# Segment mean of ten million sorted rows on one core: two junk tiles in turn for VectorE's products and for ScalarE's id sums

## The chip, the cores and the metric

One core of a Trainium2 chip runs the whole kernel. The metric is the device time of one execution in microseconds (us), the median of several runs. Of the engines, VectorE (DVE), ScalarE (ACT) and GpSimd (POOL) do the work; TensorE (PE) has six small matmuls; SyncE (SP) only issues transfers.

## The reference, cut to what matters

```python
data: 10,000,000 float32;  segment_ids: 10,000,000 int64, sorted, in 0..9999
sums[s]   = sum of data where segment_ids == s
counts[s] = number of rows where segment_ids == s
return sums / max(counts, 1)          # 10,000 float32
```

## The kernel before, in words

The data are laid out as 128 partitions of 78,125 rows. Each partition's stretch is cut into 90 rows of L = 875 elements, and since the ids are sorted and a segment holds some 1,000 elements, the kernel takes it that each such row holds at most one change of segment (a check at the end leads to a general path otherwise). So it need not read all ids. It needs, for each row, the place KK where the segment changes; of the first row of a pair the sum ahead of that place (A), of the second row the sum behind it (B), and the total of the pair (T). What lies between the two places is T - A - B.

The stages, which all run beside each other:

- **Loads.** SyncE's queue issues 45 data tiles `data_t` of two rows each (L225; 875 KB, 16 buffers) and, among them, probes: single ids at every 175th place (L213, L218).
- **First look** (`first_look`, L361 to L421, and for the odd pairs `bridge`, L483 to L526), on VectorE. From the probes it works out a window of ids that must hold the change, and writes its offset into IDX (L405, L521). Rows come in groups; PLAN holds for each group the step after which each of its parts runs, by hand.
- **Gathers** (`gather`, L345), on GpSimd's queue. 90 indirect transfers bring 175 or 232 ids per partition into one of 18 slots of the tile GT. Six gathers of a group go out one after the other.
- **Id sums** (`add_ids`, L431), on ScalarE. One activation over the gathered ids with an accumulator: its sum goes to GS, and the products themselves, which nobody reads, go to a junk tile. On the chip it is two instructions: ACTIVATE and ACTIVATION_READ_ACCUMULATOR.
- **Second look** (`second_look` L441, `bridged` L534), on VectorE. KK from GS.
- **Row totals** (`total`, L559), on ScalarE, the same form over both rows of a data tile: 45 of them, the accumulator to T, the unused products to `junk_a`.
- **Row splits** (`split`, L568), on VectorE. One scalar_tensor_tensor per row compares a ramp with KK, multiplies by the data and accumulates: the sum goes to A or B, and the unused products to `junk_v`. There are 90 of them, again two instructions each: SCALAR_TENSOR_TENSOR and DVE_READ_ACCUMULATOR.
- **The rest**: some 300 small VectorE operations (counts, scans, tables of the outputs, checks), some large ones on GpSimd, and a last part for the late rows (L1093 to L1159), which ends with the output's transfers (L1173).

The order on each engine is written out by hand: the main loop (L1280 to L1308) goes through the 90 splits, and behind each split it issues the small operations that PLAN and POS put there. So splits stand directly behind each other in some places and have one to thirteen small operations between them in others. Id sums and totals are laid among each other on ScalarE in the same loop. `need` and `mark` only check that order when the program is built.

The waits come from the framework: it notes what each instruction reads and writes, and lets an instruction wait on a semaphore for the earlier ones it must follow, also for those of its own engine. In the kernel before, every split writes `junk_v` from column 0 on, so each one follows the split before it; every id sum and every total (and the verdict's sum at L833) writes `junk_a` from column 0 on, so each one follows the one before it, of whichever kind.

Of the kernel before, what the change touches and what calls it, by code (L numbers as in the profile page):

```python
# [10 lines left out]
BF16 = mybir.dt.bfloat16  # L11
# [3 lines left out]
ACT = mybir.ActivationFunctionType  # L15
AX = mybir.AxisListType

P = 128
D = 78125
L = 875  # L20
# [6 lines left out]
WO = 232  # L27
# [149 lines left out]
def kernel(  # L177
# [16 lines left out]
    cpool = ctx.enter_context(tc.tile_pool(name="cpool", bufs=1))  # L194
# [37 lines left out]
    V, BT, KK, A, B = (q5[:, i, PAD:] for i in range(5))  # L232
    GT = gpool.tile([P, RING, WO], I64, name="GT")
    gt32 = GT.bitcast(I32)

    def view(ap, dims):
        return bass.AP(ap.tensor, ap.offset, [list(ap.ap[0])] + dims)

    nc.scalar.activation(  # L239
        out=gt32[:, :, 0 : 2 * WO : 2], in_=view(q5[:, 0, 0:1], [[0, RING], [0, WO]]), func=ACT.Copy  # L240
    )

# [6 lines left out]
    iota = ppool.tile([P, 1024], FP32, name="iota")  # L249
# [21 lines left out]
        out=plast, in0=pc, scalar1=float(P - 1), scalar2=1.0e6, op0=ALU.is_equal, op1=ALU.mult  # L271
# [5 lines left out]
        out=sp_i, in0=sp_i, scalar1=3, scalar2=None, op0=ALU.arith_shift_right  # L277
# [36 lines left out]
    RR = cpool.tile([P, NOD], FP32, name="RR")  # L314
    DD = cpool.tile([P, NOD], FP32, name="DD")
    uu = cpool.tile([P, 2 * NOD], FP32, name="uu")
    junk_v = cpool.tile([P, L], BF16, name="junk_v")
    junk_a = cpool.tile([P, 2 * L], BF16, name="junk_a")

    def own(t, i, j):  # L320
        return view(t[:, 4 * i : 4 * i + 1], [[4, j - i], [1, 2]])

    def odd(t, i, j):
        return view(t[:, 4 * i + 2 : 4 * i + 3], [[4, j - i], [1, 2]])
# [7 lines left out]
    slots, queue, made = {}, [], set()  # L332

    def mark(what, rows):
        made.update((what, r) for r in rows)

    def need(what, rows):
        assert all((what, r) in made for r in rows), (what, [r for r in rows if (what, r) not in made])
# [89 lines left out]
    def add_ids(r):  # L428
        mark('GS', [r])
        w = W if r % 4 < 2 else WO  # L430
        nc.scalar.activation(  # L431
            out=junk_a[:, 0:w], in_=gt32[:, slots[r], 0 : 2 * w : 2], func=ACT.Copy,
            accum_out=GS[:, r : r + 1],
        )

# [127 lines left out]
    def split(r):  # L563
        need('KK', [r])
        mark('A', [r])
        n = min(L, D - r * L)
        d = tiles[r // 2][:, (r % 2) * L : (r % 2) * L + n]
        nc.vector.scalar_tensor_tensor(  # L568
            out=junk_v[:, 0:n], in0=iota[:, 0:n], scalar=KK[:, r : r + 1], in1=d,
            op0=ALU.is_ge if r % 2 else ALU.is_lt, op1=ALU.mult,  # L570
            accum_out=(B if r % 2 else A)[:, r : r + 1],
        )
# [707 lines left out]
    for s in range(-60, NR):  # L1280
        while pnext < len(pieces) and pieces[pnext][2] <= s + X_DATA:
            f, a, _ = pieces[pnext]
            f(*a)
            pnext += 1
        while nt < NT and 2 * nt <= s + X_DATA:
            load_data(ORDER[nt])
            nt += 1
        if s == -X_DATA:
            nc.scalar.dma_start(
                out=snt[0 : P - 1, :],  # L1290
                in_=segment_ids[D : N].rearrange("(p d) -> p d", d=D)[:, 0:1],
            )
        if s == -1:
            for f in after[s][:head]:
                f()
        if s >= -1:
            for r in sums_at[s]:
                add_ids(r)
        if s == -1:
            for f in after[s][head:]:  # L1300
                f()
        if s >= 0:
            r = SEQ[s]
            for t in totals_at[s]:
                total(t)
            split(r)
            for f in after[s]:
                f()  # L1308
# [31 lines left out]
```

## Time and profile before

| | |
|---|---|
| median of 3 runs | 185.46 us (185.43, 185.46, 188.05) |
| the profiled execution | 185.97 us, of which its span is 184.2 us |
| VectorE busy | 141.4 us (77%), 479 instructions |
| ScalarE busy | 132.8 us (72%), 291 instructions |
| GpSimd busy | 115.8 us (63%), 176 instructions |
| row splits L568 | 90 x 1117 ns, and 90 reads of the accumulator x 82 ns |
| id sums L431 | 90 x 384 ns, and 90 reads x 187 ns |
| row totals L559 | 45 x 1650 ns, and 45 reads x 186 ns |
| moved by DMA | 56.69 MB, mean 308 GB/s |

Times in the rows are counted from the start of the span. A line such as L568 is the line of the kernel that issued the instruction. In a timeline, the first number is the start, the second the duration in us, and a bracket at the end is the idle time of the engine just before and what ended it. [...] A wait that ends while an earlier record of the same engine runs on doesn't show as idle.

### The profile page before, as it was taken

Reading aid. Unit: us, or ns where it says so; the run is one execution under the profiler, and the core shown is the slowest. Engines: PE = TensorE matmul, PEld = TensorE weight load, DVE = VectorE, ACT = ScalarE, POOL = GpSimd, SP = SyncE. Lnnn points to the kernel's source line nnn. Section 1 sums busy time; section 2 is a strip of 40 time slices with the busy share of each in tenths; the row PEclk is TensorE's granted clock in tenths of the full one; section 3 lists DMA queues with packets and bytes.
Section 4 is the critical chain, followed back from the end, with each engine's and each line's share of the span. In section 5 each row is a group of like instructions: output and inputs, shape, how many; then the busy total and the mean of one; then the engine's idle time right before and its main releaser. Section 6 shows DMA issues by size and latency. Waiting matters only on the chain.

```text
span 184.2 us, 1506 instructions
## 1 busy us (share of the span) xinstructions
PE 1.6 (1%) x6; PEld 1.4 (1%) x6; DVE 141.4 (77%) x479; ACT 132.8 (72%) x291; POOL 115.8 (63%) x176
## 2 busy tenths in 40 slices
PE   0000000000000000020000000000000000000100
PEld 0000000000000000020000000000000000000100
DVE  6404385820899995769967999979999999999990
ACT  8903566654899996959957949679988687996410
POOL 5476777778585776876773857468628579245700
DMA  5899999999999999999999999999999999950000
GB/s 120 118 289 263 165 251 370 299 405 338 391 351 331 372 373 342 403 254 398 347 350 395 344 350 384 364 410 412 410 405 415 414 403 412 409 240 0 0 0 12
DMA packets 47684, 56.69 MB, mean 308 GB/s; under 512 B 37664, under 2 KB 38104, under 8 KB 47671
## 3 DMA queue, kind: packets, MB, share of 16 engines
q1 hardware_dynamic: 41739, 40.32, 66.3%
q0 software_dynamic: 5760, 16.26, 25.2%
q14 instruction: 13, 0.11, 0.2%
q10 hardware_dynamic: 172, 0.00, 0.1%
HBM read 58.97 MB, written 0.04 MB: 320 GB/s over the span
## 4 chain that ended last, share of the span: by engine, by line
DMA 33%; DVE 27%; issue 25%; POOL 7%; ACT 5%; POOLq 0%; DVEq 0%; ACTq 0%
DMA GT<-in_segment_ids_dram,IDX 18%; DVE junk_v L568 15%; DMA data_t<-in_data_dram 15%; POOL GT L345 5%; ACT junk_a L431 3%; ACT junk_a L559 2%; DVE q L587 1%; DVE most L1135 1%; DVE pa L1022 0%; POOL i_i L250 0%; DVE shf L988 0%; DVE xa L998 0%; DVE FFP L887 0%; DVE bad L725 0%; DVE q L590 0%
## 5 line engine op out<-in xcount | busy, mean ns | idle before, releaser
L345 POOL DMA_INDIRECT GT<-in_segment_ids_dram,IDX x90 | 91.0, 1011 | 44.1 <-issue 26.0
L568 DVE SCALAR_TENSOR_TENSOR junk_v<-iota,q,data_t 128x875 bf16<-128x875 f32 x90 | 100.6, 1117 | 3.4 <-DMA data_t<-in_data_dram 2.7
L559 ACT ACTIVATE junk_a<-data_t 128x1750 bf16<-128x1750 f32 (+1 forms) x45 | 74.3, 1650 | 7.2 <-DMA data_t<-in_data_dram 5.1
L431 ACT ACTIVATE junk_a<-GT 128x175 bf16<-128x175 int32 (+1 forms) x90 | 34.6, 384 | 30.6 <-DMA GT<-in_segment_ids_dram,IDX 26.3
L431 ACT ACTIVATION_READ_ACCUMULATOR junk_a<-GT 128x1 f32 x90 | 16.8, 187 | 0.0
L441 DVE SCALAR_TENSOR_TENSOR q<-YY,GS 128x6 f32<-128x6 f32 (+2 forms) x9 | 1.5, 170 | 13.8 <-ACT junk_a L431 13.0
L534 DVE TENSOR_TENSOR q<-ZV,GS 128x6 f32<-128x6 f32 (+1 forms) x8 | 1.3, 160 | 10.7 <-ACT junk_a L431 10.7
L559 ACT ACTIVATION_READ_ACCUMULATOR junk_a<-data_t 128x1 f32 x45 | 8.4, 186 | 0.0
L568 DVE DVE_READ_ACCUMULATOR junk_v<-iota,q,data_t 128x1 f32 x90 | 7.4, 82 | 0.0
L361 DVE TENSOR_TENSOR q<-pr 128x12 f32<-128x12 int32 (+3 forms) x9 | 1.6, 176 | 4.8 <-DMA pr<-in_segment_ids_dram 4.8
L239 ACT ACTIVATE GT<-q 128x4176 int32<-128x4176 f32 x1 | 3.9, 3899 | 0.0
L833 ACT ACTIVATE junk_a<-bad 128x272 bf16<-128x272 f32 x1 | 0.4, 429 | 4.3 <-DVE bad L814 4.3
L1038 POOL TENSOR_TENSOR xa<-pa,RG 128x720 f32<-128x720 f32 x1 | 1.6, 1630 | 1.9 <-DVE RG L1034 1.9
L1090 POOL TENSOR_TENSOR pb<-pb,RB 128x620 f32<-128x620 f32 x1 | 1.3, 1302 | 2.4 <-DVE RB L875 2.4
L1058 POOL TENSOR_TENSOR xa<-xa 128x36 f32<-128x36 f32 (+3 forms) x5 | 2.3, 469 | 0.3
L548 POOL TENSOR_TENSOR uu<-uu,GS 128x44 f32<-128x44 f32 x1 | 0.3, 278 | 3.5 <-ACT junk_a L431 3.5
L457 POOL TENSOR_SCALAR LN<-NBP 128x6 f32<-128x6 f32 (+1 forms) x8 | 1.6, 199 | 1.2 <-issue 0.7
L464 POOL TENSOR_TENSOR FB<-FB,wb 128x6 f32<-128x6 f32 (+1 forms) x8 | 1.8, 228 | 0.7
L470 POOL TENSOR_TENSOR WV<-wb,WV 128x6 f32<-128x6 f32 (+1 forms) x8 | 1.6, 205 | 0.7
L461 POOL TENSOR_SCALAR FB<-NBP 128x6 f32<-128x6 f32 (+1 forms) x8 | 1.6, 198 | 0.6
L1025 POOL TENSOR_SCALAR pb<-pb 128x620 f32<-128x620 f32 x1 | 1.8, 1771 | 0.1
L526 DVE TENSOR_TENSOR ZV<-IDX,WV 128x6 f32<-128x6 int32 (+1 forms) x8 | 1.3, 165 | 0.7
(162 smaller groups left out, 81.3 us busy)
## 6 DMA issues: line engine op xcount, KB each, us to landing
data_t<-in_data_dram SPq DMA_DIRECT2D x44, 875.0 KB
GT<-in_segment_ids_dram,IDX POOLq DMA_INDIRECT x90
data_t<-in_data_dram SPq DMA_DIRECT2D x1, 562.5 KB
pr<-in_segment_ids_dram SPq DMA_DIRECT2D x22, 11.0 KB
pr<-in_segment_ids_dram SPq DMA_DIRECT2D x3, 6.0 KB
out_dram<-OUT SPq DMA_DIRECT2D x1, 36.6 KB
pr<-in_segment_ids_dram SPq DMA_DIRECT2D x1, 4.0 KB
snt<-in_segment_ids_dram ACTq DMA_DIRECT2D x1, 1.0 KB
```

The lines of the kernel that those rows point to most:

```text
L239: nc.scalar.activation(out=gt32[:, :, 0 : 2 * WO : 2], in_=view(q5[:, 0, 0:1], [[0, RING], [0, WO]]), func=ACT.Copy)
L345: nc.gpsimd.indirect_dma_start(out=GT[:, slots[r], 0:w], out_offset=None, in_=ids2d[:], in_offset=bass.IndirectOffsetOnAxis(ap=IDX[:, r : ...
L361: nc.vector.tensor_sub(out=BT[:, a:b], in0=VI[:, a + 1 : b + 1], in1=VI[:, a:b])
L431: nc.scalar.activation(out=junk_a[:, 0:w], in_=gt32[:, slots[r], 0 : 2 * w : 2], func=ACT.Copy, accum_out=GS[:, r : r + 1],)
L457: e.tensor_scalar(out=own(LN, i, j), in0=own(NB, i, j), scalar1=-1024.0 * FAR, scalar2=-3.0 * L, op0=ALU.mult, op1=ALU.add,)
L464: e.tensor_tensor(out=o(FB), in0=o(FB), in1=o(wb), op=ALU.add)
L559: nc.scalar.activation(out=junk_a[:, 0:n], in_=tiles[t][:, 0:n], func=ACT.Copy, accum_out=T[:, 2 * t : 2 * t + 1])
L568: nc.vector.scalar_tensor_tensor(out=junk_v[:, 0:n], in0=iota[:, 0:n], scalar=KK[:, r : r + 1], in1=d, op0=ALU.is_ge if r % 2 else ALU.is_ ...
L587: nc.vector.tensor_sub(out=odd(A), in0=even(T), in1=even(A))
L1025: e.tensor_scalar(out=o, in0=o, scalar1=0.0, scalar2=None, op0=ALU.is_equal)
L1058: nc.gpsimd.tensor_tensor(out=m[:, :, 0 : w - h], in0=m[:, :, 0 : w - h], in1=m[:, :, h:w], op=ALU.add)
L1135: nc.vector.tensor_reduce(out=most, in_=add, axis=AX.X, op=ALU.add)
```

## The change

Three things change. `junk_v` becomes two tiles of the same size, and each split takes the other one than the split before it. The id sums get two tiles of their own, `junk_i`, 232 wide, and take them in turn in the same way. The row totals (and the verdict's sum) keep `junk_a`. `turned` turns the list of two round while the program is being built and gives the first; it leaves no instruction.

```diff
+    def turned(two):
+        two.reverse()
+        return two[0]
+
...
-    junk_v = cpool.tile([P, L], BF16, name="junk_v")
+    junk_v = [cpool.tile([P, L], BF16, name=f"junk_v{k}") for k in (0, 1)]
+    junk_i = [cpool.tile([P, WO], BF16, name=f"junk_i{k}") for k in (0, 1)]
     junk_a = cpool.tile([P, 2 * L], BF16, name="junk_a")
...
         nc.scalar.activation(
-            out=junk_a[:, 0:w], in_=gt32[:, slots[r], 0 : 2 * w : 2], func=ACT.Copy,
+            out=turned(junk_i)[:, 0:w], in_=gt32[:, slots[r], 0 : 2 * w : 2], func=ACT.Copy,
             accum_out=GS[:, r : r + 1],
         )
...
         nc.vector.scalar_tensor_tensor(
-            out=junk_v[:, 0:n], in0=iota[:, 0:n], scalar=KK[:, r : r + 1], in1=d,
+            out=turned(junk_v)[:, 0:n], in0=iota[:, 0:n], scalar=KK[:, r : r + 1], in1=d,
             op0=ALU.is_ge if r % 2 else ALU.is_lt, op1=ALU.mult,
             accum_out=(B if r % 2 else A)[:, r : r + 1],
         )
```

## Rows read from the trace of the kernel before

**Rows 1.** Stretches: busy us of each engine, TensorE clock, DMA share, GB/s.

```profile
48.00:93.80 45.80, 0.99 (x4) 0.93 (x4) 38.34 (x113) 39.83 (x88) 32.60 (x47) 1.00 1.05 356
...
124.30:164.00 39.70, 0.00 (x0) 0.00 (x0) 39.00 (x141) 35.22 (x71) 23.70 (x33) 1.00 1.01 406
164.00:179.30 15.30, 0.59 (x2) 0.50 (x2) 14.97 (x34) 7.21 (x17) 7.28 (x12) 1.00 0.02 7
```

**Rows 2.** Whom VectorE waits for from 114.6 us on: total us, times, longest.

```profile
DVE q L441 <- ACT junk_a L431: 1.2, 1, 1.2
DVE junk_v L568 <- DMA data_t<-in_data_dram: 0.3, 1, 0.3
```

**Rows 3.** Timeline of VectorE: splits that wait for data.

```profile
93.77 1.13 DVE L568 SCALAR_TENSOR_TENSOR junk_v<-iota,q,data_t 128x875 bf16<-128x875 f32 x1 [1.56 <-DMA data_t<-in_data_dram]
...
101.09 1.13 DVE L568 SCALAR_TENSOR_TENSOR junk_v<-iota,q,data_t 128x875 bf16<-128x875 f32 x1 [0.92 <-DMA data_t<-in_data_dram]
...
114.51 1.13 DVE L568 SCALAR_TENSOR_TENSOR junk_v<-iota,q,data_t 128x875 bf16<-128x875 f32 x1 [0.26 <-DMA data_t<-in_data_dram]
```

**Rows 4.** Timelines of VectorE, GpSimd, ScalarE, VectorE: the chain to the last group.

```profile
109.11 0.17 DVE L405 SCALAR_TENSOR_TENSOR IDX<-ST,wb 128x6 int32<-128x6 f32 x1
...
110.04 1.08 POOL L345 DMA_INDIRECT GT<-in_segment_ids_dram,IDX  x1 [0.70 <-issue]
...
123.85 0.36 ACT L431 ACTIVATE junk_a<-GT 128x175 bf16<-128x175 int32 x1 [0.70 <-DMA GT<-in_segment_ids_dram,IDX]
...
124.34 0.17 DVE L441 SCALAR_TENSOR_TENSOR q<-YY,GS 128x6 f32<-128x6 f32 x1 [1.20 <-ACT junk_a L431]
```

**Rows 5.** Timeline of VectorE: a split behind a split, then L910.

```profile
102.15 0.08 DVE L568 DVE_READ_ACCUMULATOR junk_v<-iota,q,data_t 128x1 f32 x1
102.27 1.13 DVE L568 SCALAR_TENSOR_TENSOR junk_v<-iota,q,data_t 128x875 bf16<-128x875 f32 x1
103.32 0.08 DVE L568 DVE_READ_ACCUMULATOR junk_v<-iota,q,data_t 128x1 f32 x1
103.32 0.17 DVE L910 TENSOR_TENSOR psx<-rp,q 128x20 f32<-128x20 f32 x1
```

**Rows 6.** Timeline of VectorE: small operations, one and two between splits.

```profile
128.36 0.16 DVE L490 SCALAR_TENSOR_TENSOR LL<-LK 128x3 f32<-128x3 f32 x1
128.43 0.16 DVE L873 TENSOR_TENSOR RB<-q,ct 128x10 f32<-128x10 f32 x1
...
175.00 0.08 DVE L568 DVE_READ_ACCUMULATOR junk_v<-iota,q,data_t 128x1 f32 x1
175.00 0.15 DVE L840 TENSOR_SCALAR badi<-small 128x1 int32<-128x1 f32 x1
175.12 1.13 DVE L568 SCALAR_TENSOR_TENSOR junk_v<-iota,q,data_t 128x875 bf16<-128x875 f32 x1
```

**Rows 7.** Timeline of VectorE: the splits that are counted, first and last ones.

```profile
50.79 1.13 DVE L568 SCALAR_TENSOR_TENSOR junk_v<-iota,q,data_t 128x875 bf16<-128x875 f32 x1
...
129.68 1.13 DVE L568 SCALAR_TENSOR_TENSOR junk_v<-iota,q,data_t 128x875 bf16<-128x875 f32 x1
...
156.03 1.13 DVE L568 SCALAR_TENSOR_TENSOR junk_v<-iota,q,data_t 128x875 bf16<-128x875 f32 x1
...
173.95 1.13 DVE L568 SCALAR_TENSOR_TENSOR junk_v<-iota,q,data_t 128x875 bf16<-128x875 f32 x1
```

**Rows 8.** Timeline of ScalarE: a sum behind a sum, and a product behind a sum.

```profile
99.80 0.19 ACT L431 ACTIVATION_READ_ACCUMULATOR junk_a<-GT 128x1 f32 x1
100.02 0.36 ACT L431 ACTIVATE junk_a<-GT 128x175 bf16<-128x175 int32 x1
...
173.18 0.18 ACT L833 ACTIVATION_READ_ACCUMULATOR junk_a<-bad 128x1 f32 x1
173.28 0.34 ACT L1146 ACTIVATE add<-ga,q 128x31 f32<-128x31 f32 x1
```

**Rows 9.** DMA queue of the 90 gathers: packets, MB, share of 16 engines.

```profile
q0 software_dynamic: 5760, 16.26, 25.2%
```

## The prediction

> **What bounds the kernel now.** I read the stretches first. From 48 us to 164 us the DMA engines never rest: their share is 1.05 at 356 GB/s up to 93.8 us and 1.01 at 406 GB/s from 124.3 us on [rows 1]. The reader is to see what changes between the two: in the second stretch VectorE is busy 39.00 of 39.70 us, and from 164 us, with the DMA share down to 0.02, still 14.97 of 15.30 us. So the last 55 us, 124.3 to 179.3, are VectorE's, and the transfers end some 15 us ahead of it.
>
> Next I read whom VectorE waits for. From 114.6 us on there are two entries in all, 1.2 us for ScalarE's id sums and 0.3 us for a data tile [rows 2], whose wait began before the window. Before that it is different: at 93.77 us a split starts after 1.56 us of waiting for its data tile, at 101.09 after 0.92, and at 114.51 after 0.26 us [rows 3]. Whatever VectorE gains ahead of such a wait only makes the wait longer, as long as the data comes when it did.
>
> The 1.2 us wait ends at 124.34 us in the second look of the last group. Behind it stands a chain [rows 4]: VectorE writes the offsets IDX at 109.11 + 0.17 = 109.28 us, the first of six gathers of the group starts on GpSimd 0.76 us later, at 110.04, the others follow one by one, and the last id sum starts at 123.85 us after ScalarE had idled 0.70 us for its gather. ScalarE's own speed isn't in this wait: it was idle before the sum.
>
> **The change part by part.** No instruction is added or dropped, no step is moved and no byte is transferred more. Two junk tiles taken in turn only move the wait for a product to be overwritten: from the instruction just before to the one two before, or off the row total for ScalarE's sums.
>
> *A split right behind a split.* The read of the accumulator starts at 102.15 us, and the next split at 102.27, 0.12 us later and 0.04 us behind that read's end [rows 5]. Behind the next split the read starts at 103.32 and an instruction that needs nothing of the split, L910, at 103.32 as well. So the wait costs up to 0.12 us, nearly all of it hidden from the idle column, since the 0.08 us read counts as busy. The trace has no accumulating instruction that follows a split without such a wait, so the bounds are nothing and 0.12 us. A loss is excluded for this edit by itself: what the split waits for after the change was done before what it waits for now. I take 0.12, from L910, the only row of an instruction that follows a split unheld.
>
> [...]
>
> *A split one small operation behind a split.* At 175.00 us the read and L840 start together, the split at 175.12 [rows 6]: the wait for the read still binds. Small operations that don't wait follow at 0.07 us (128.36 to 128.43 in the same rows), so the split could start at 175.07 or 175.08; bounds nothing and 0.05 us, I take 0.04. With two or more operations between, the read is long done and nothing is gained.
>
> *How many are on the path.* In the whole trace 16 splits start 0.12 us behind the read of the split directly before them, the first at 50.79 and the last at 173.95 us; but only two of the 16, at 156.03 and 173.95, come after 124.34 us [rows 7]. There the other checks and sums fill the places between splits. Six more have one small operation between, from 129.68 us [rows 7] to 175.12 us [rows 6]. The gain on the path behind 124.34 us is 2 x 0.12 + 6 x 0.04 = 0.48 us; bounds 0 and 2 x 0.12 + 6 x 0.05 = 0.54 us.
>
> *The 14 earlier ones.* All but one lie ahead of the split that waits for data at 101.09 us or of the one at 93.77 us [rows 3], and what they give goes into those waits. The split at 102.27 us [rows 5] lies behind the last of them that matters to the chain of rows 4: IDX at 109.11 comes up to 0.12 us earlier, and so do the gathers and the wait's end at 124.34. Bounds nothing and 0.12, I take 0.10, since VectorE works without a long wait from 102.27 to 109.11 us.
>
> *ScalarE.* Today a sum starts 0.22 us behind the start of the read before it (99.80 to 100.02), while the first product of the late rows, which has no such wait, starts 0.10 us behind it (173.18 to 173.28) [rows 8]. That is 0.12 us for each sum, and for each row total behind a sum; for 90 sums and at most 44 totals up to 134 x 0.12 = 16 us of ScalarE's time, bounds nothing and that. Two totals in a row keep their wait. On the path I count it as nothing: the only wait of VectorE for ScalarE in the last 70 us ends with a sum before which ScalarE was idle [rows 2, 4]. Its cover is the gathers' landing; if that cover were gone the 1.2 us of rows 2 would be the most it could bring. Earlier, sums that end sooner let VectorE write IDX sooner and gathers start sooner; the data wait at 93.77 us takes that back.
>
> *The sum.* 0.48 + 0.10 = 0.58 us, say 0.6. The profiled execution took 185.97 us, with a span of 184.2 and 1.8 us around it, so it would take 185.4. It stands 0.5 us above the median of the runs, 185.46; on that scale the time is 185.46 - 0.6 = 184.9 us. What is late next is VectorE still: the last data is there when VectorE still has 15 us to do [rows 1], and no other engine is waited for.
>
> **The rivals.**
>
> *The hold isn't the wait (no gain).* Two accumulating instructions might not overlap with the read between them, whatever the semaphores. Then splits start 0.12 us behind the read after the change too, and only what ScalarE's 0.12 us bring is left: 185.3 to 185.5 us. For it: no row shows an unheld accumulating follower. Against it: L910 [rows 5], and that L840's follower waits as long for a read that is one operation back [rows 6]. [...]
>
> *The earlier splits count in full.* If the head weren't set by the data's coming but by VectorE's own pace, all 16 splits would count, and the two with one operation between in the head: 16 x 0.12 + 8 x 0.04 = 2.2 us, so 183.2 us. For it: VectorE also waits for id sums in the head, behind gathers that its own IDX starts, as in rows 4. Against it: 1.56 us of waiting for data at 93.77 us [rows 3], and a DMA share of 1.05 before it [rows 1], so the data can't come sooner.
>
> *Gathers go ahead of the data (slower).* With VectorE and ScalarE ahead in the head, gathers start earlier and take DMA time from the data tiles for which the splits wait at 93.77, 101.09 and 114.51 us. One gather is 16.26 MB / 90 = 0.18 MB [rows 9], which takes 0.51 us at 356 GB/s [rows 1]. Each one that comes to stand ahead of the tile of 114.51 us moves the whole VectorE stretch by 0.51 us. One such gather costs 0.1 us less than the 0.6 gained; from two on the kernel is slower, by 2 x 0.51 - 0.6 = 0.4 us: 185.9 us. For it: the DMA engines are full, so an earlier gather must displace something. Against it: VectorE's whole gain in the head is 14 x 0.12 us, under 2 us, so hardly more than one gather can come earlier, and by 114.5 us the same gathers are due in both versions.
>
> **How the numbers follow.** The forecast, 184.9 us with its own range from 184.6 to 185.3, has 0.55; no gain on VectorE, 185.4, has 0.22; the full head, 183.2, has 0.08; gathers ahead, 185.9, has 0.12; 0.03 is left for what I don't see. The range that reaches into the full head on one side and past two gathers and the scatter between the runs on the other is 183.7 to 186.2 us. A measurement of this kernel tells about 2%, 3.7 us, from no change; none of the cases reaches 181.8 or 189.2 us. So faster has 0.03, same 0.94 and slower 0.03.
>
> **What would show it.** Right: in the timeline of VectorE a split behind a split starts with the read of the accumulator or within 0.03 us of it, on ScalarE the step from a read to the next sum goes from 0.22 to about 0.10 us, and the busy time of both hardly moves while ScalarE idles more for gathers and data. The wait for data at 93.77 us grows, the second look at 124.34 us starts at about 124.2, and the last split starts 0.6 us earlier than 177.82 us. Wrong on the price: the 0.12 us stay between splits. Wrong on the place: VectorE's data waits between 93 and 115 us end earlier or later by more than 0.5 us; then the order of gathers and data set the time, and the difference between the two versions there is carried to the end.

## The result and the profile after

The changed kernel took 186.76 us, the median of 20 runs (185.61 to 188.94); the kernel before, 20 runs beside it, 185.35 us. The ratio is 1.0073 with a 95% interval from 1.0044 to 1.0101. So the change is a loss of 0.7%, some 1.4 us, inside the 2% that one would call "same", but outside the forecast's range (183.7 to 186.2 us) and with the wrong sign. A second set of runs of the changed kernel gave 1.0069. Comparisons leave disturbed (slower) runs out, and of the two experiments whose profile was disturbed, e1 and h4, no packet time is used.

The profiled execution of the changed kernel took 187.62 us, its span 185.8. The page's busy times and its DMA queues:

```profile
PE 1.6 (1%) x6; PEld 1.4 (1%) x6; DVE 140.1 (75%) x479; ACT 124.1 (67%) x291; POOL 115.9 (62%) x176
...
q1 hardware_dynamic: 41739, 40.32, 66.2%
q0 software_dynamic: 5760, 16.26, 25.8%
```

ScalarE is busy 8.7 us less than before and VectorE 1.3 us less, with the same instructions: busy time counts overlapping records once (of records that sum to 147 us before and 146 us after on ScalarE, 132.8 and 124.1 us are busy; on VectorE, of 171 and 170 us, 141.4 and 140.1), and a read of the accumulator now runs beside the instruction behind it (16 reads of 0.08 us are VectorE's 1.3 us). The prediction had said that both hardly move. The bytes and packets are the same too; but the gathers' packets (q0) took 25.8% of a longer span, 47.9 us, where [rows 9] had 25.2% of 184.2, 46.4 us.

What was forecast for the instructions is there. Timeline of VectorE, changed kernel:

```profile
95.94 1.13 DVE L573 SCALAR_TENSOR_TENSOR junk_v<-iota,q,data_t 128x875 bf16<-128x875 f32 x1 [1.41 <-DMA data_t<-in_data_dram]
...
103.19 1.13 DVE L573 SCALAR_TENSOR_TENSOR junk_v<-iota,q,data_t 128x875 bf16<-128x875 f32 x1 [0.80 <-DMA data_t<-in_data_dram]
104.25 0.08 DVE L573 DVE_READ_ACCUMULATOR junk_v<-iota,q,data_t 128x1 f32 x1
104.25 1.13 DVE L573 SCALAR_TENSOR_TENSOR junk_v<-iota,q,data_t 128x875 bf16<-128x875 f32 x1
105.30 0.08 DVE L573 DVE_READ_ACCUMULATOR junk_v<-iota,q,data_t 128x1 f32 x1
...
126.38 0.17 DVE L446 SCALAR_TENSOR_TENSOR q<-YY,GS 128x6 f32<-128x6 f32 x1 [0.87 <-ACT junk_i L436]
...
176.66 0.08 DVE L573 DVE_READ_ACCUMULATOR junk_v<-iota,q,data_t 128x1 f32 x1
176.66 0.15 DVE L845 TENSOR_SCALAR badi<-small 128x1 int32<-128x1 f32 x1
176.73 1.12 DVE L573 SCALAR_TENSOR_TENSOR junk_v<-iota,q,data_t 128x875 bf16<-128x875 f32 x1
...
180.58 0.27 DVE L1164 SCALAR_TENSOR_TENSOR OUT<-gb,q,most 128x31 f32<-128x31 f32 x1
```

The pair of [rows 5] is at 104.25 us now: the second split starts with the read of the first, where it came 0.12 us behind it. The pair with one small operation between ([rows 6], 175.00 to 175.12 us) went from 0.12 to 0.07 us (176.66 to 176.73). Timeline of ScalarE, changed kernel, the place of [rows 8]:

```profile
101.33 0.35 ACT L436 ACTIVATE junk_i<-GT 128x175 bf16<-128x175 int32 x1
101.58 0.18 ACT L436 ACTIVATION_READ_ACCUMULATOR junk_i<-GT 128x1 f32 x1
101.67 0.34 ACT L436 ACTIVATE junk_i<-GT 128x175 bf16<-128x175 int32 x1
```

A sum starts 0.09 us behind the read before it, not 0.22. And the last stretch is shorter as forecast. It begins with the second look that ended the wait of [rows 4], at 126.38 us now, and runs to the start of the last operation on the output (180.58 us): 54.20 us; before, from 124.34 us [rows 4] to 178.99 us, it took 54.65 us. (Rows 4 and the prediction call this look the last group's. It is the last but one's, of six rows; the last group's, of four rows, comes at 143.66 us in the kernel before, without a wait. The sums don't hang on the name.)

But that stretch begins 2.04 us later. The stretches that answer to [rows 1], and whom VectorE waits for, in the changed kernel:

```profile
48.00:95.97 47.97, 0.98 (x4) 0.93 (x4) 37.55 (x115) 37.02 (x89) 32.56 (x47) 1.00 1.06 358
126.38:166.00 39.62, 0.00 (x0) 0.00 (x0) 39.00 (x142) 33.13 (x70) 24.13 (x33) 1.00 1.01 404
166.00:181.00 15.00, 0.59 (x2) 0.50 (x2) 14.60 (x33) 6.82 (x17) 7.05 (x12) 1.00 0.03 14
```

```profile
DVE junk_v L573 <- DMA data_t<-in_data_dram: 5.9, 4, 3.0
```

The end is VectorE's, as before. By "the head" is meant all that lies ahead of the last stretch. There VectorE waits 5.9 us for data tiles in four waits (2.7 us in three before), but the longest of the four replaces another wait and costs nothing. Before:

```profile
74.30 0.17 DVE L534 TENSOR_TENSOR q<-ZV,GS 128x6 f32<-128x6 f32 x1 [2.77 <-ACT junk_a L431]
```

The changed kernel at the same place:

```profile
73.29 1.13 DVE L573 SCALAR_TENSOR_TENSOR junk_v<-iota,q,data_t 128x875 bf16<-128x875 f32 x1 [3.02 <-DMA data_t<-in_data_dram]
...
74.35 0.16 DVE L539 TENSOR_TENSOR q<-ZV,GS 128x6 f32<-128x6 f32 x1
```

So at 74.35 us VectorE is level with before, and the delay arises behind that: the split that waited until 93.77 us [rows 3] waits until 95.94 us. This one profile lies 0.9 us above the kernel's median, so it can't say by how much the data came late. A second profile of the same kernel (the run f4 below) took 185.31 us, 1.1 us under the median of its runs, and has the look at

```profile
124.27 0.17 DVE L446 SCALAR_TENSOR_TENSOR q<-YY,GS 128x6 f32<-128x6 f32 x1 [1.11 <-ACT junk_i L436]
```

Each profile set on its own kernel's median, an estimate, the look comes at 123.7 us before and at 125.5 and 125.4 us in the two profiles of the changed kernel, 1.7 to 1.8 us later. What can be compared from one profile to the next is the packet time: the durations of all packets in the trace, summed, over 16 engines. It was 169.2 us before, 171.7 us in this profile of the changed kernel and 170.6 us in the second one, for the same packets.

### The profile page after: what moved, and what is told of

Same layout as the page of the kernel before. It is cut to its first block, busy times and chain, and to the rows that moved or that the text cites. A ratio compares the mean times of both kernels' runs of the same rounds, so it can differ in the third digit from the quotient of the medians.

```text
span 185.8 us, 1458 instructions
## 1 busy us (share of the span) xinstructions
PE 1.6 (1%) x6; PEld 1.4 (1%) x6; DVE 140.1 (75%) x479; ACT 124.1 (67%) x291; POOL 115.9 (62%) x176
## 3 DMA queue, kind: packets, MB, share of 16 engines
q1 hardware_dynamic: 41739, 40.32, 66.2%
q0 software_dynamic: 5760, 16.26, 25.8%
## 4 chain that ended last, share of the span: by engine, by line
DMA 34%; DVE 26%; issue 19%; POOL 12%; ACT 5%; POOLq 0%; DVEq 0%; ACTq 0%
DMA GT<-in_segment_ids_dram,IDX 21%; DVE junk_v L573 17%; DMA data_t<-in_data_dram 14%; POOL GT L350 9%; ACT junk_a L564 4%; ACT junk_i L436 2%; DVE q L592 1%; DVE most L1140 1%; POOL i_i L254 0%; DVE shf L993 0%; POOLq L350 0%; POOL WV L475 0%; POOL FB L469 0%; POOL LN L462 0%; POOL FB L466 0%
## 5 line engine op out<-in xcount | busy, mean ns | idle before, releaser
L573 DVE SCALAR_TENSOR_TENSOR junk_v<-iota,q,data_t 128x875 bf16<-128x875 f32 x90 | 99.5, 1116 | 7.2 <-DMA data_t<-in_data_dram 5.9
L436 ACT ACTIVATE junk_i<-GT 128x175 bf16<-128x175 int32 (+1 forms) x90 | 33.6, 374 | 36.8 <-DMA GT<-in_segment_ids_dram,IDX 35.2
L436 ACT ACTIVATION_READ_ACCUMULATOR junk_i<-GT 128x1 f32 x90 | 16.8, 187 | 0.0
```

The lines of the kernel that those rows point to most:

```text
L436: nc.scalar.activation(out=turned(junk_i)[:, 0:w], in_=gt32[:, slots[r], 0 : 2 * w : 2], func=ACT.Copy, accum_out=GS[:, r : r + 1],)
L573: nc.vector.scalar_tensor_tensor(out=turned(junk_v)[:, 0:n], in0=iota[:, 0:n], scalar=KK[:, r : r + 1], in1=d, op0=ALU.is_ge if r % 2 else ...
```

## The experiments

Two theories. *Order*: VectorE and ScalarE are earlier in the head, so gathers and loads are issued in another order or rhythm and spoil each other (the rival of the prediction, in a larger form). *Place*: the three added tiles lie ahead of most other tiles in SBUF and move all of them by 2720 bytes. In the program as built, GT, where the gathers land, goes from byte 184576 of each partition, a multiple of 64, to 187296, 32 bytes past one; its slots are 1856 = 29 x 64 bytes apart, so all 18 are off. The 16 data buffers, 7008 bytes apart, are in turn on and 32 past a multiple of 64, and those two halves change roles.

All runs, in one table; the sections below give edits and expectations. Every kernel computes the whole of the reference. "Turned" says what takes two tiles in turn; "GT" is its start past a multiple of 64; the ratio is to the kernel before, run beside it on the same chip; the last stretch is measured as above.

| run | turned | GT | ratio [95% interval] | packet time, us | last stretch, us |
|---|---|---|---|---|---|
| before | none | 0 | 1 | 169.2 | 54.65 |
| the change | both | 32 | 1.0073 [1.0044, 1.0101] | 171.7 | 54.20 |
| e1 | none | 32 | 1.0034 [0.9997, 1.0070] | | 54.59 |
| e2 | both | 0 | 0.9988 [0.9949, 1.0028] | 169.6 | 54.09 |
| e3 | none | 32 | 1.0033 [0.9996, 1.0071] | 170.9 | 54.57 |
| e4 | both | 0 | 1.0003 [0.9963, 1.0042] | 169.6 | 54.00 |
| f1 | splits | 0 | 0.9983 [0.9951, 1.0014] | 169.0 | 54.11 |
| f2 | sums | 0 | 1.0010 [0.9973, 1.0048] | 169.3 | 54.60 |
| f3 | both, pitch 7040 | 0 | 1.0044 [1.0011, 1.0078] | 170.4 | 54.02 |
| f4 (the change again) | both | 32 | 1.0069 [1.0031, 1.0107] | 170.6 | 53.99 |
| g1 | none, pitch 7040 | 0 | 0.9954 [0.9919, 0.9989] | 168.4 | 54.59 |
| g2 | none | 0 | 1.0024 [0.9990, 1.0057] | 169.1 | 54.60 |
| g3 | none | 8 | 1.0023 [0.9994, 1.0051] | 170.0 | 54.69 |
| g4 | both, pitch 7072 | 0 | 1.0026 [0.9991, 1.0060] | 169.4 | 54.13 |
| h1 | none | 32 | 1.0073 [1.0045, 1.0101] | 171.1 | 54.65 |
| h2 | both | 0 | 1.0004 [0.9977, 1.0032] | 169.2 | 53.99 |
| h3 | splits, pitch 7040 | 0 | **0.9935 [0.9908, 0.9963]** | 168.4 | 54.07 |
| h4 | both, pitch 7040 | 0 | 0.9963 [0.9932, 0.9994] | | 54.03 |
| i1 | none | 0 | 1.0001 [0.9978, 1.0024] | 169.1 | 54.61 |
| i2 | splits, pitch 7040 | 32 | 1.0011 [0.9984, 1.0037] | 169.9 | 54.15 |

**Moving all tiles, or GT alone, by 32 bytes.** e1 (before) and e2 (the change) make `junk_a` 32 bytes wider, which moves everything behind it:

```diff
-    junk_a = cpool.tile([P, 2 * L], BF16, name="junk_a")
+    junk_a = cpool.tile([P, 2 * L + 16], BF16, name="junk_a")
```

> The kernel before with junk_a 32 bytes wider and nothing else, so that every tile allocated behind it (the data tiles, GT) lies 32 bytes further, as it does to a multiple of 64 bytes in the changed kernel; every instruction and wait as before. Address theory (the new tiles push GT from a multiple of 64 bytes to 32 bytes past one, and the gathers then take longer: 25.8% of 185.8 us against 25.2% of 184.2 in the two profiles): slower than before by about 2.0 us, the 1.4 measured and the 0.6 forecast as a gain, ratio near 1.010. Order theory (the earlier id sums and splits change the order of gathers and data, and the data of the head comes 2 us later): as before, ratio 1.000 within 0.002.

> The changed kernel with junk_a 32 bytes wider and nothing else, so that the data tiles and GT lie as in the kernel before to a multiple of 64 bytes; every instruction and wait as in the changed kernel. Address theory: the loss goes and the forecast gain is left, 0.4 to 0.6 us faster than before, ratio near 0.997. Order theory: as the changed kernel, ratio near 1.007.

e3 (before) and e4 (the change) leave 32 bytes free ahead of GT, so that GT alone moves (and the few tiles behind it):

```diff
-    GT = gpool.tile([P, RING, WO], I64, name="GT")
-    gt32 = GT.bitcast(I32)
+    GTW = gpool.tile([P, RING * WO + 4], I64, name="GT"); GT = GTW[:, 4:].rearrange("p (r w) -> p r w", w=WO)
+    gt32 = GTW.bitcast(I32)[:, 8:].rearrange("p (r w) -> p r w", w=2 * WO)
```

> The kernel before with GT alone 32 bytes further (a wider tile of which the first four ids are left unused); the data tiles and all else where they were. If GT's place is what counts: as the first of these runs, about 2 us slower, ratio near 1.010. If the data tiles' place counts, or the order: ratio 1.000 within 0.002.

> The changed kernel with GT alone 32 bytes further, which brings it back to a multiple of 64 bytes; the data tiles stay where the change put them. If GT's place is what counts: ratio near 0.997, as the second of these runs. If the data tiles' place counts, or the order: as the changed kernel, ratio near 1.007.

With GT off a multiple of 64 the kernel before got to 1.0034 and 1.0033, with intervals that just touch 1; with GT back on one the changed kernel got to 0.9988 and 1.0003. All four lean to place, and e3 and e4, where the data buffers didn't move, to GT. The size was missed: of e1 and e3 place had expected about 1.010, and a third of that came.

**One part of the change alone, GT on a multiple of 64.** f1 turns the splits alone (and widens `junk_a` by 32 bytes for GT's sake), f2 the sums alone:

```diff
 f1, against the change:
-    junk_i = [cpool.tile([P, WO], BF16, name=f"junk_i{k}") for k in (0, 1)]
-    junk_a = cpool.tile([P, 2 * L], BF16, name="junk_a")
+    junk_a = cpool.tile([P, 2 * L + 16], BF16, name="junk_a")
...
-            out=turned(junk_i)[:, 0:w], in_=gt32[:, slots[r], 0 : 2 * w : 2], func=ACT.Copy,
+            out=junk_a[:, 0:w], in_=gt32[:, slots[r], 0 : 2 * w : 2], func=ACT.Copy,
 f2, against the change:
-    junk_v = [cpool.tile([P, L], BF16, name=f"junk_v{k}") for k in (0, 1)]
+    junk_v = cpool.tile([P, L], BF16, name="junk_v")
...
-            out=turned(junk_v)[:, 0:n], in0=iota[:, 0:n], scalar=KK[:, r : r + 1], in1=d,
+            out=junk_v[:, 0:n], in0=iota[:, 0:n], scalar=KK[:, r : r + 1], in1=d,
```

> Only the splits take two junk tiles in turn; the id sums stay with junk_a, and junk_a is 32 bytes wider, so that the data tiles and GT lie as before to a multiple of 64 bytes. Address theory (the loss of the change came from GT's place alone, the waits act as forecast): the VectorE stretch from the last second look to the end is 0.5 us shorter than the 54.6 us of before, and the time with it, ratio near 0.997. Order theory (sums that end earlier on ScalarE let gathers get ahead of the data): also 0.997, since ScalarE is as before.

> Only the id sums take two tiles of their own; the splits stay with one junk tile; the data tiles and GT lie as before to a multiple of 64 bytes without any padding. Address theory: the stretch from the last second look to the end stays at 54.6 us and the time at before, ratio 1.000 within 0.002. Order theory: the data of the head comes later, 0.3 to 0.6 us, ratio near 1.003.

f1 0.9983, f2 1.0010: neither part loses the 0.7% of the change. The 0.3% that order had expected of f2 is not excluded, since its interval reaches to 1.0048. The last stretch tells whose gain it is: 54.11 us with the splits, 54.60 us with the sums. As forecast, the sums bring nothing to the end.

f3 takes the changed kernel with data buffers 7040 bytes apart instead of 7008 and `junk_a` 32 bytes wider, so that all buffers and GT start on multiples of 64; f4 is the changed kernel again.

```diff
-        d = dpool.tile([P, 2 * L], FP32, name="data_t")
+        d = dpool.tile([P, 2 * L + 8], FP32, name="data_t")
```

> The changed kernel with junk_a 32 bytes wider and each data tile's buffer 40 bytes further from the next, so that GT and all 16 data buffers start at a multiple of 64 bytes (in every kernel up to now every second data buffer starts 32 bytes past one); instructions and waits of the changed kernel. If the data tiles' place costs like GT's: the packets' time of the loads' queue falls and the time too, 0.5 us or more below the kernel before, ratio 0.995. If only GT's place counts: as the second run, ratio 0.997 to 1.000.

> The changed kernel as it is, on the same chip as the three runs beside it. Address theory: ratio 1.004 to 1.010, the transfers' packets take 1.3 us or more longer in all 16 engines than where GT starts at a multiple of 64 bytes, and the last second look starts later than in the other three. Order theory: the same ratio, but then the run with the sums alone is slower too.

f4 repeats the loss (1.0069). f3 is a miss for the plain form of the place theory: everything on multiples of 64, and still 1.0044.

**Other places.** g1 is the kernel before with f3's edit of the data buffers alone; g2 widens `junk_a` of before by 64 bytes; g3 moves GT of before by 8 bytes, in the way of e3; g4 is the changed kernel with `junk_a` 32 bytes wider and data buffers `2 * L + 16` wide (7072 bytes apart).

```diff
 g2, against before:
-    junk_a = cpool.tile([P, 2 * L], BF16, name="junk_a")
+    junk_a = cpool.tile([P, 2 * L + 32], BF16, name="junk_a")
 g3, against before:
-    GT = gpool.tile([P, RING, WO], I64, name="GT")
+    GTW = gpool.tile([P, RING * WO + 4], I64, name="GT"); GT = GTW[:, 1 : RING * WO + 1].rearrange("p (r w) -> p r w", w=WO)
...
 g4, against the change, with junk_a as in e2:
-        d = dpool.tile([P, 2 * L], FP32, name="data_t")
+        d = dpool.tile([P, 2 * L + 16], FP32, name="data_t")
```

> The kernel before with each data tile's buffer 40 bytes further from the next, so that all 16 data buffers start at a multiple of 64 bytes; GT stays at one; instructions and waits of before. If it was the data buffers' even spacing that made the run with everything at multiples of 64 slower: ratio near 1.005, packets in all 1 us longer in the 16 engines than the 169.2 us of before. If the place of the data buffers counts for nothing: 1.000 within 0.003 and 169 to 169.6 us.

> The kernel before with junk_a 64 bytes wider: all behind it moves by 64 bytes, so GT still starts at a multiple of 64. Address theory with multiples of 64 as what counts: nothing, ratio 1.000 within 0.003, packets 169 to 169.6 us. [...]

> The kernel before with GT alone 8 bytes further, one id. Address theory, if what costs is a row of gathered ids that starts inside a block of 64 bytes: as with 32 bytes, ratio 1.003 to 1.008, packets 170.5 us or more. If what costs is the distance of 32 bytes itself: ratio 1.000 and packets below 170 us.

> The changed kernel with junk_a 32 bytes wider and the data buffers 72 bytes further apart than in the change, so that every second one starts 32 bytes past a multiple of 64 again, with gaps between them as wide as in the run with everything at multiples of 64; GT at a multiple of 64. If the even spacing made that run slower: back to 0.997 to 1.000, packets below 169.7 us. If it was the gaps or the higher place of GT: near 1.004 again, packets above 170 us.

g1, with the instructions of before, is faster than before, 0.9954, clear of 1, which neither expectation had: GT's start past a multiple of 64 isn't the only place that matters. Whether it is the data buffers' isn't separated, since GT lies behind the 16 buffers and moves with them by 16 x 32 = 512 bytes. g2, g3 and g4 can't be told from 1; g3 and g4 lie between what their two cases expected and decide nothing.

**Instructions and places crossed.** h1 has the old instructions at the new places: the three tiles are taken as in the change and never written. h2 has the new instructions at the old places: the three tiles are taken in a pool behind all others, so that GT and the data buffers lie as before (which tile takes which of five of the buffers differs).

```diff
 h1, against before:
-    junk_v = cpool.tile([P, L], BF16, name="junk_v")
+    junk_v = [cpool.tile([P, L], BF16, name=f"junk_v{k}") for k in (0, 1)][0]
+    junk_i = [cpool.tile([P, WO], BF16, name=f"junk_i{k}") for k in (0, 1)]
 h2, against the change:
+    xpool = ctx.enter_context(tc.tile_pool(name="xpool", bufs=1))
...
-    junk_v = [cpool.tile([P, L], BF16, name=f"junk_v{k}") for k in (0, 1)]
-    junk_i = [cpool.tile([P, WO], BF16, name=f"junk_i{k}") for k in (0, 1)]
+    junk_v = [t.tile([P, L], BF16, name=f"junk_v{k}") for k, t in enumerate((cpool, xpool))]
+    junk_i = [xpool.tile([P, WO], BF16, name=f"junk_i{k}") for k in (0, 1)]
```

> The kernel before with the three tiles that the change adds taken in the same places and never written, so that GT (187296, 32 bytes past a multiple of 64) and all 16 data buffers lie where they lie in the changed kernel, while every instruction is that of before. Place theory (the tiles' places slow the transfers): slower than before by what the changed kernel lost plus the 0.5 us that its splits gained, so a ratio of 1.007 to 1.011, and a sum of packet times above 170.5 us. Order theory (what VectorE and ScalarE do earlier in the head spoils the order of the transfers, places don't matter): the kernel before, ratio 0.998 to 1.002.

> The changed kernel with the three added tiles taken behind all others, so that GT (184576) and the 16 data buffers lie where they lie in the kernel before. Place theory: only the gain of the splits is left, 0.5 us, ratio 0.995 to 0.999. Order theory: as slow as the changed kernel, ratio 1.005 to 1.010.

h1 has not one instruction of the change and the whole of its loss, 1.0073. h2 has all the instructions and no loss, 1.0004; its interval ends at 1.0032, below what order expected. The order theory is out as the cause of the loss. h2 is not the gain that place expected, though (0.995 to 0.999): with the places alike, the instructions of the change bring nothing. What that says is taken up below.

h3 is h2's placing with the splits alone turned, h4 the whole of h2, both with f3's edit of the data buffers:

```diff
 h3, against before, with the change's split:
-    junk_v = cpool.tile([P, L], BF16, name="junk_v")
+    junk_v = [t.tile([P, L], BF16, name=f"junk_v{k}") for k, t in enumerate((cpool, xpool))]
...
-        d = dpool.tile([P, 2 * L], FP32, name="data_t")
+        d = dpool.tile([P, 2 * L + 8], FP32, name="data_t")
```

> The kernel before with the splits alone turned, their second tile behind all others, and data buffers of 7040 instead of 7008 bytes' pitch, so that all other tiles lie as in the run of before with that pitch (ratio 0.995). Place theory: both gains add up, 0.995 x 0.997 = 0.992, range 0.989 to 0.995. Order theory: the turned splits move the head as they did in the changed kernel, ratio 0.998 or more.

> The whole change with its three added tiles behind all others and the pitch of 7040 bytes. Place theory: as the splits alone, 0.989 to 0.995, since ScalarE's shorter waits are not on the path. Order theory with ScalarE's sums as its cause: slower than the run with the splits alone by 0.5% or more. The earlier run of the change with this pitch, which lay 2752 bytes further on, had 1.004; if this one has that too, it isn't the place but the sums with the pitch.

h3 is the fastest of all, 183.63 us, 0.9935: the places of g1 (0.9954) and the splits' gain add up. h4, 0.9963, lies between what the two theories expected.

**Which tile's place.** i1 is h1 with GT alone moved by 32 bytes, to a multiple of 64; i2 is h3 with GT alone moved by 32 bytes, off one. The edit is that of e3.

> The run h1 (old instructions, every tile at the changed kernel's places: 1.0073) with GT alone moved 32 bytes on, to a multiple of 64 (187328); the data buffers stay at the changed kernel's places. If GT's place is the cause: the kernel before, ratio 0.998 to 1.003, packet times back to about 169.3 us. If it is the data buffers' places: 1.005 to 1.010 as h1, packet times above 170.5 us.

> The fastest run, h3 (splits alone turned, pitch 7040, GT on a multiple of 64: 0.9935), with GT alone moved 32 bytes on, off a multiple of 64. If GT's place costs what the run of before with GT alone moved showed (0.3%) up to what h1 showed (0.7%): ratio 0.996 to 1.001 and packet times 1 to 2 us above h3's 168.4. If GT's place costs nothing by itself: 0.992 to 0.995.

i1 1.0001, i2 1.0011. In i1 the whole loss of h1 is gone, in i2 the whole gain of h3, by 32 bytes of one tile: 0.72% and 0.76%, the same step at two sets of places of the data buffers and with two sets of instructions. With e4, where the same 32 bytes take the changed kernel from 1.0073 to 1.0003, three pairs say that it is GT's place that costs the changed kernel its time. A few small tiles behind GT (in i2 the splits' second junk tile too) move with it; only engines use them, no transfer lands there. h1 and h3 ran on another chip than i1 and i2, each beside the kernel before.

How that looks in the profiles: stretches of h1, old instructions, new places, GT 32 past a multiple of 64 (busy us of each engine, clock, DMA share, GB/s):

```profile
31.00:48.00 17.00, 0.00 (x0) 0.00 (x0) 7.46 (x28) 8.74 (x26) 13.04 (x14) 1.00 1.06 345
48.00:125.00 77.00, 0.98 (x4) 0.93 (x4) 65.91 (x208) 63.10 (x143) 51.32 (x76) 1.00 1.05 355
```

The same stretches of i1, GT on a multiple of 64:

```profile
31.00:48.00 17.00, 0.00 (x0) 0.00 (x0) 7.29 (x29) 8.55 (x27) 12.96 (x13) 1.00 1.06 352
48.00:125.00 77.00, 0.99 (x4) 0.93 (x4) 68.16 (x216) 65.36 (x145) 52.73 (x77) 1.00 1.06 363
```

Of h3, GT on a multiple of 64:

```profile
48.00:125.00 77.00, 0.99 (x4) 0.93 (x4) 67.29 (x221) 65.51 (x143) 53.10 (x77) 1.00 1.06 364
```

Of i2, GT 32 past one:

```profile
48.00:125.00 77.00, 0.98 (x4) 0.93 (x4) 64.97 (x211) 63.57 (x143) 51.96 (x76) 1.00 1.05 358
```

The DMA engines are as full in the one as in the other (1.05 and 1.06), and move 2% less, 355 against 363 and 358 against 364 GB/s, while VectorE gets through 8 to 10 fewer instructions in the same 77 us. By itself this is weak: over all the runs this stretch has 355 to 365 GB/s with GT on a multiple of 64 (358 in f1, 359 in h2) and 355 to 360 with it 32 past. The packet time separates them: at a pitch of 7008 bytes it is 169.0 to 169.6 us with GT on a multiple of 64 and 170.6 to 171.7 us with it 32 past; at 7040 bytes and the old places 168.4 and 169.9 us. Only f3 stands apart, with 170.4 us and GT on a multiple of 64. Then the second look with which the last stretch begins. h1:

```profile
125.25 0.17 DVE L442 SCALAR_TENSOR_TENSOR q<-YY,GS 128x6 f32<-128x6 f32 x1 [1.03 <-ACT junk_a L432]
...
179.90 0.27 DVE L1160 SCALAR_TENSOR_TENSOR OUT<-gb,q,most 128x31 f32<-128x31 f32 x1
```

i1:

```profile
122.69 0.17 DVE L442 SCALAR_TENSOR_TENSOR q<-YY,GS 128x6 f32<-128x6 f32 x1 [0.37 <-ACT junk_a L432]
...
177.31 0.27 DVE L1160 SCALAR_TENSOR_TENSOR OUT<-gb,q,most 128x31 f32<-128x31 f32 x1
```

From there on both take 54.6 us: the whole difference is made in the head, where the transfers set the pace. Whose packets got longer? Part 3 of the page, h1:

```profile
q1 hardware_dynamic: 41739, 40.32, 66.2%
q0 software_dynamic: 5760, 16.26, 25.9%
```

and i1:

```profile
q1 hardware_dynamic: 41739, 40.32, 66.5%
q0 software_dynamic: 5760, 16.26, 25.9%
```

Of spans of 185.1 and 182.5 us that is 47.9 against 47.3 us for the gathers and 122.5 against 121.4 us for the loads. Both got longer, the loads, whose tiles didn't move, as well as the gathers. Why a start off a multiple of 64 does this isn't shown by any run.

## Why the prediction was wrong

*A split behind a split, 0.12 us, and one operation between, 0.04 us: right.* At 104.25 us the first shows in full, at 176.66 us the second with 0.05. L910 [rows 5] was not the only instruction that followed a split unheld, as the prediction has it (L840 in [rows 6] starts beside the read too), but the reading was right. In the changed kernel the next split, an accumulating instruction, starts together with the 0.08 us read (104.25 us for both), and the rival *no gain on VectorE* falls with it.

*The last stretch, 0.48 us: right.* In the eleven kernels with turned splits it takes 53.99 to 54.20 us, mean 54.07; in the nine without, 54.57 to 54.69 us, mean 54.62. That is 0.55 us, just past the upper bound of 0.54. From that operation to the span's end the kernels with turned splits take 5.27 us and the others 5.20 or 5.21, so 0.48 us of it reach the end.

*ScalarE, 0.12 us for each sum and nothing on the path: right at the end.* It measured 0.22 - 0.09 = 0.13 us for each, and f2's last stretch, with the sums alone turned, is that of before.

*The head, 0.10 us of gain: wrong, and here the forecast fell.* The steps that failed are the sentence "Two junk tiles taken in turn only move the wait for a product to be overwritten" and the condition "as long as the data comes when it did". The two `junk_i` and the second `junk_v` also move every tile allocated behind them, and with GT 32 bytes past a multiple of 64 the data didn't come when it did. The missing term is h1 against i1: 0.72% of 185 us, 1.3 us.

*And the head's other half: wrong as well.* At equal places the change should still have brought its 0.6 us, 0.3%. Four pairs have the old and the new instructions at the same places: the change against h1 0.00%, e4 against i1 +0.02%, h2 against before +0.04%, h4 against g1 +0.09%. Their mean, weighted by the intervals, is +0.04% with ±0.19%, an estimate that leaves -0.3% outside. Since 0.48 us are gained behind the head, the head must have given about 0.5 us back, where the prediction had it gain 0.10. With both terms the sum is 1.3 + 0.5 - 0.5 = 1.3 us of loss; measured were 0.73%, 1.4 us. Why the new instructions cost the head something is open: gathers and loads may come in another order, and the kernels, as built, also differ in which data tile takes which of five buffers. The splits alone lean to a gain (f1 -0.17%, h3 against g1 -0.19%), the sums to a cost (f2 against before +0.10%, h2 against f1 +0.21%, h4 against h3 +0.28%), each within its interval. So the order theory is out for the 1.3 us, but in a small form no run excludes it.

*The rivals.* The full head (183.2 us) didn't come: the head got longer. *Gathers ahead of the data* forecast 185.9 us and the right sign, for a reason that h1 rules out as the main one: the loss is there with gathers issued by the old instructions. The prediction's own sign of error, data waits of VectorE between 93 and 115 us that end more than 0.5 us off, showed in the first profile of the changed kernel (93.77 to 95.94 us) and not in f4's, where that wait ends at 93.45 us. The sign laid it to the order of gathers and data; for the main part the runs put GT's place there.

## What to carry to other kernels

A new tile, though nobody reads it, moves the tiles allocated behind it; before the time of a changed instruction is judged, run the old instructions with the new tiles in place and unused, and the new ones with their tiles behind all others. Where transfers set the pace, look at the start of the tiles on which they land: 32 bytes were worth more here (0.7%) than what the splits gain behind the head (0.3%), and the whole change of the instructions was worth nothing at equal places. The version to keep is h3: the splits alone turned, the second tile behind all others, and data buffers 7040 bytes apart, 0.9935 [0.9908, 0.9963] of before.

## What the runs showed of the hardware that was not expected

- A landing place of the gathers 32 bytes past a multiple of 64 cost 0.7% here, where 90 gathers of 16.26 MB in all run among 40.32 MB of loads: h1 to i1 0.72%, i2 to h3 0.76%, the change to e4 0.70%. With before's other places it was less, 0.33% (e3) and 0.23% (8 bytes past, g3), with intervals that still hold 1, so the difference from 0.7% isn't clear of noise either. The packets in all took 2.0 us (h1 against i1) and 1.5 us (i2 against h3) longer on the mean of the 16 engines; in h1 against i1 those of the loads too, 122.5 against 121.4 us.
- Multiples of 64 aren't all of it. Data buffers 7040 bytes apart, with GT 512 bytes further on, gave 0.46% at the old places (g1; h3 against f1 0.48%, h4 against h2 0.41%), but in f3, where the same buffers and GT lay 2752 bytes further on, the kernel was at 1.0044. What tells f3 from h4 stays open.
- One profile can mislead about the head. The two profiles of the changed kernel differ by 2.3 us, and most of that arises in 9 us. The changed kernel's first profile:

```profile
22.00:31.00 9.00, 0.00 (x0) 0.00 (x0) 4.94 (x23) 5.22 (x17) 6.80 (x12) 1.00 0.93 232
```

and its second, f4:

```profile
22.00:31.00 9.00, 0.00 (x0) 0.00 (x0) 6.26 (x29) 6.23 (x18) 6.58 (x13) 1.00 1.08 336
```

  That is 104 GB/s x 9 us = 0.94 MB less, some 2.6 us at 356 GB/s [rows 1], from the same program. Of all packets together the two profiles have 171.7 and 170.6 us. So the medians carry the verdict here, with the packet times beside them, not the data waits of one profile.
